# Hybrid diffusion layer on one core: gate loads issued ahead, two buffers for the S5 output rows, a freer engine choice for weight low parts

## The chip, the cores and the metric

The kernel runs on one core of a Trainium2 chip. The metric is the device time of one launch in microseconds. Three runs of the kernel before gave 1892.18, 1900.79 and 1914.18 us, median 1900.79 us. The engines are named as in the profile: PE (TensorE matmul), PEld (its weight loads), DVE (VectorE), ACT (ScalarE), POOL (GpSimd), and SP (SyncE), whose queue issues the DMAs; SPq is that queue.

## The reference, cut to what matters

One layer over 512 latent tokens with a context of 256 tokens, width 1024: half-step SwiGLU FFN, then two token mixers side by side (a bidirectional S5 state-space scan and a bidirectional RWKV-7), merged by per-channel gates, then a second half-step FFN and a final RMSNorm. The part around the change:

```python
xs = scan of h[c] = a * h[c-1] + x[c]            # S5, both directions
ya = (ya_f + ya_b) + p['s5_D'] * u
ya = jax.nn.gelu(ya)
ya = ya * jax.nn.sigmoid(ya @ p['s5_w_glu'])
...
yb = (yb * g) @ p['rwkv_w_o']
merged = jax.nn.sigmoid(gate_a) * (ya @ p['s5_w_proj']) + jax.nn.sigmoid(gate_b) * yb
return merged @ p['w_out']
x = x + mod_x[5] * out_x
```

## The kernel before, in words

**Products in three parts.** Every dense weight block of 128 x 1024 floats is loaded as `raw`, rounded by ACT into a high part `wh`, and the rest `wl = raw - wh` is formed by DVE or POOL. Activations are held the same way (for instance `yg`, `ya`, `yb`, `hx`, each a pair). `mm3` then issues three matmuls per 128-row block: wh x high, wh x low, wl x high. The blocks form one long list `self.items`, worked off in order by the generator `dense` (line 352): split the item's weights, issue loads for free `raw` buffers, split a few items ahead (four among the products of the mixers, two elsewhere), then issue the matmuls. `w_split` (line 328) picks the engine for `wl`: from item `n_post + 2` up to `n_ffn`, which is wo, wproj and wout, always POOL; in the other items DVE where a modelled comparison (`late`) says that POOL would end later.

**The order.** All instructions are emitted by one planner (`Plan`, line 52), which models when each engine becomes free and runs a set of generators by priority: a generator gives up its turn with the list of things it next needs, and the planner resumes the first one in priority whose needs are met at its modelled PE time. So the order in each engine's queue is fixed at build time by the model; on the chip each engine works its queue strictly in that order. `dense` is the filler: it runs where nothing of higher priority is ready, or where the modelled PE work of the last stretch falls under a quota.

**Stage b2** (`phase_b2`, line 1817; about 1109 to 1332 us). Beside one another: `rw_main` and `rw_pre` (RWKV chunks 4 to 11), `rw_solve` for two groups of triangular solves on DVE (results `Tl`, `AT` stored in `ti`, read back as `T` and `tt`), `s5_rec` (line 1747), which is 63 steps of four small POOL operations on `t` and `hs`, then `s5_out` (line 1765), eight blocks of PE work (`b<-U,Tz`, `b<-hs,gt`) that store their rows to `yd` in DRAM, and the filler with the sigmoid gates: `gst` goes to `gates` in DRAM.

**After it.** `s5_post` (line 1962) reads `yd` back tile by tile into `yi` (one buffer), applies the gelu into `ga` and splits it into `yg`. `glu_mm` (line 1888) needs all four `yg` tiles and gives `ya`. Four gate items stand behind it in the list. Then come sixteen items of two products each, one product being 12 matmuls of 256 columns into one PSUM bank: `wo_mm` for the first half of the tokens (reads `yb`), `proj_mm` for the first half (reads `ya`), then both for the second half. Each product loads its gate tile `gt` (128 x 256) from `gates` just before its matmuls are issued; `gt` has two buffers. DVE multiplies it with the bank (`gb` for wo, `gt` itself for wproj); for wproj it also adds `gb`, ACT rounds to the high part of `hx`, and DVE subtracts for the low part. The products rotate over four PSUM banks. `wout_mm` follows from `hx`. The second FFN starts near 1500 us.

Of the kernel before, what the change touches and what calls it, by code (L numbers as in the profile page):

```python
# [8 lines left out]
F32 = mybir.dt.float32  # L9
# [274 lines left out]
class Kern:  # L284
# [43 lines left out]
    def w_split(self):  # L328

        nc, i = self.nc, self.n_split  # L330
        if i == len(self.items):
            return
        s = next((s for s in self.slots if i < self.end[s[0]]), None)
        if s is None:
            return
        if i not in self.raw:
            self.w_loads(1)
        self.n_split += 1
        nb = self.items[i][1]
        r, sr = self.raw.pop(i)  # L340
        self.slots.remove(s)
        wh, wl = (s[0].tile([128, 8, 128], F32R, name=n, tag=f"{n}{s[1]}") for n in ("wh", "wl"))
        nc.scalar.copy(wh[:, :nb], r[:, :nb])
        f = self.sch.free
        late = max(f["P"], self.sch.t) + 2300 > max(f["V"], self.sch.t) + 1150
        eng = nc.vector if (i < self.n_post + 2 or i >= self.n_ffn) and late else nc.gpsimd
        eng.tensor_sub(wl[:, :nb], r[:, :nb], wh[:, :nb].bitcast(F32))
        if sr[0] not in self.gone:
            self.raws.append(sr)
        self.wsp[i] = (wh, wl, s)  # L350
# [48 lines left out]
    def build(self):  # L399
        nc, tc, a, es = self.nc, self.tc, self.a, self.es  # L400
        self.X, self.C = X, C = Reg(0, NX, 4), Reg(1, NCT, 0)
        self.raw, self.wsp, self.n_load, self.n_split, self.late = {}, {}, 0, 0, None
        self.slots, self.raws, self.gone, self.end, self.items = [], [], set(), {}, []
        per = es.enter_context(self.pool("per"))
# [46 lines left out]
        i = self.n_gate + GATE0  # L451
# [1295 lines left out]
    def s5_rec(self, r):  # L1747

        Pg, h = self.nc.gpsimd, r.hs
        yield [f"s5in{r.s}"]  # L1750
        if not r.v:
            Pg.tensor_copy(h[:, 0], self.s5e)
        for c in range(1, 32 if r.v else 64):
            t1 = r.sp.tile([128, 2, 32], F32, name="t1")
            t2 = r.sp.tile([128, 2, 32], F32, name="t2")
            Pg.tensor_mul(t1, self.arr, h[:, c - 1])
            Pg.tensor_mul(t2, self.aii, h[:, c - 1, ::-1])
            Pg.tensor_add(t1, t1, h[:, c])
            Pg.tensor_add(h[:, c], t1, t2)
            yield [("P", RECP)]  # L1760
        if r.v:
            Pg.tensor_copy(self.s5e, h[:, 31])
        self.sch.post(f"s5rec{r.s}")
# [106 lines left out]
    def dbank(self):  # L1870
        self.alt += 1
        return self.bank(self.dbanks[self.alt % len(self.dbanks)])

    def wo_mm(self, h, t, wh, wl):
        nc, c = self.nc, self.X.half[h]
        for e in range(2):
            d = 2 * t + e
            yield [f"yb{h}2", f"yb{h}3"]
            yield [self.yb[1][:, :, c]]
            g = self.cp.tile([128, 256], F32, name="gt", bufs=2)  # L1880
            nc.sync.dma_start(g, self.gates[8 + d][:, c])
            px = self.dbank()[:, 0:256]
            for k in range(4):
                self.mm3(px, wh[:, e * 4 + k], wl[:, e * 4 + k], self.yb[0][:, k, c], self.yb[1][:, k, c], k == 0, k == 3)
                yield
            nc.vector.tensor_mul(self.gb[:, d], g, px)
# [19 lines left out]
    def proj_mm(self, h, t, wh, wl):  # L1906
        nc, cp, c, late = self.nc, self.cp, self.X.half[h], None
        for e in range(2):
            d = 2 * t + e
            g = cp.tile([128, 256], F32, name="gt", bufs=2)  # L1910
            nc.sync.dma_start(g, self.gates[d][:, c])
            px = self.dbank()[:, 0:256]
            for k in range(4):
                self.mm3(px, wh[:, e * 4 + k], wl[:, e * 4 + k], self.ya[0][:, k, c], self.ya[1][:, k, c], k == 0, k == 3)
                yield
            nc.vector.tensor_mul(g, g, px)
            nc.vector.tensor_add(g, g, self.gb[:, d])
            hi, lo = (x[:, d, c] for x in self.hx)
            nc.scalar.copy(hi, g)
            if late:  # L1920
                nc.vector.tensor_sub(*late)
            late = lo, g, hi.bitcast(F32)
            if e:
                nc.vector.tensor_sub(*late)
# [37 lines left out]
    def s5_post(self, pb):  # L1962

        nc = self.nc
        yield ["yd3", "sv"]
        self.sos.close()
        self.s5s.close()
        self.c1 = c = pb.enter_context(self.pool("c1"))
        R = lambda n: [c.tile([128, 4, NX], F32R, name=f"{n}{i}") for i in range(2)]
        self.ga, self.yg, self.ya, self.yb = c.tile([128, 4, NX], F32, name="ga"), R("yg"), R("ya"), None  # L1970
        for t in range(4):
            yi = c.tile([128, 8, 64], F32, name="yi", bufs=1)
            nc.sync.dma_start(yi, self.yd[t].rearrange("(t o) g c -> (o g) t c", o=16))
            yield [yi]
            for o, i, n in ((0, 16, 48), (48, 0, 16)):
                nc.scalar.activation(self.ga[:, t, o * 8:(o + n) * 8].rearrange("p (c t) -> p c t", t=8),
                                     yi[:, :, i:i + n].rearrange("p t c -> p c t"), AF.Gelu_apprx_tanh)
            self.hl(c, self.ga[:, t], self.yg[0][:, t], self.yg[1][:, t])
            self.sch.post(f"yg{t}")
# [159 lines left out]
```

## Time and profile before

| what | value |
|---|---|
| median of three runs | 1900.79 us (1892.18 to 1914.18) |
| profiled execution, its own time | 1891.72 us |
| its span, first to last instruction | 1890.0 us |
| PE busy | 1672.3 us (88%) |
| DVE / ACT / POOL busy | 996.4 / 716.9 / 687.5 us |
| mean granted PE clock | 0.939 of full speed |
| chain that ended last | PE 56%, DVE 14%, DMA 14%, ACT 6%, issue 4% |

A row of the chain of waits gives its start, its length, and the engine or DMA that held it. A row of a timeline gives start, length, engine, operation and tiles, and in brackets how long the engine stood idle before it and what released it. Nearly all instructions carry one line number, that of the helper that records them (L209), so rows are told apart by tile names.

### The profile page before, as it was taken

Reading aid. Unit: us, or ns where it says so; the run is one execution under the profiler, and the core shown is the slowest. Engines: PE = TensorE matmul, PEld = TensorE weight load, DVE = VectorE, ACT = ScalarE, POOL = GpSimd, SP = SyncE. Lnnn points to the kernel's source line nnn. Section 1 sums busy time; section 2 is a strip of 40 time slices with the busy share of each in tenths; the row PEclk is TensorE's granted clock in tenths of the full one; section 3 lists DMA queues with packets and bytes.
Section 4 is the critical chain, followed back from the end, with each engine's and each line's share of the span. In section 5 each row is a group of like instructions: output and inputs, shape, how many; then the busy total and the mean of one; then the engine's idle time right before and its main releaser. Section 6 shows DMA issues by size and latency. Waiting matters only on the chain.

```text
span 1890.0 us, 33157 instructions
## 1 busy us (share of the span) xinstructions
PE 1672.3 (88%) x13208; PEld 1400.3 (74%) x13208; DVE 996.4 (53%) x1747; ACT 716.9 (38%) x1200; POOL 687.5 (36%) x815
## 2 busy tenths in 40 slices
PE   6889999999999988778976789968697999999996
PEld 3689987778878867665544567758587988888886
DVE  3376564755558728355788855643343433333335
ACT  3355442545463212535443333443443332222222
POOL 0144231555764314621334537660065421111111
PEclk9999999999999999888988889979799999999998
DMA  9955541335454474433753566466364223323231
GB/s 310 331 167 195 183 155 57 113 106 159 143 160 140 141 190 151 119 123 128 252 160 105 148 223 188 118 172 176 123 215 159 67 69 101 99 91 101 98 101 56
DMA packets 235626, 278.43 MB, mean 147 GB/s; under 512 B 93616, under 2 KB 186800, under 8 KB 234448
## 3 DMA queue, kind: packets, MB, share of 16 engines
q1 hardware_dynamic: 235472, 276.32, 47.8%
q8 instruction: 104, 1.70, 0.4%
q14 instruction: 50, 0.41, 0.1%
HBM read 234.31 MB, written 43.22 MB: 147 GB/s over the span
## 4 chain that ended last, share of the span: by engine, by line
PE 56%; DVE 14%; DMA 14%; ACT 6%; issue 4%; POOL 3%; SPq 3%; DVEq 0%; ACTq 0%; POOLq 0%
PE b L209 56%; DMA wmod<-in_wmod 3%; SPq L209 3%; POOL wl L209 2%; ACT wh L209 2%; DMA Hd<-H 2%; DMA raw<-in_wgu 2%; DVE st L209 1%; DVE mh L209 1%; DVE wl L209 1%; DMA gt<-gates 1%; DVE rs L209 1%; DVE prod L209 1%; DVE cvr L209 1%; DVE H L209 1%
## 5 line engine op out<-in xcount | busy, mean ns | idle before, releaser
L209 PE MATMUL b<-hx,wh 128*128 128x512 f32 (+1 forms) x2432 | 698.2, 374 | 22.6 <-ACT wh L209 10.9
L209 POOL TENSOR_TENSOR wl<-raw,wh 128x1024 fp32r<-128x1024 f32 x135 | 329.3, 2443 | 822.0 <-ACT wh L209 748.1
L209 PEld LDWEIGHTS b<-hx,wh 128*128 128x128 f32 x2432 | 439.1, 194 | 106.7 <-issue 19.0
L209 PE MATMUL b<-hx,wl 128*128 128x512 f32 (+1 forms) x1216 | 448.6, 369 | 7.6 <-POOL wl L209 6.0
L209 ACT CAST wh<-raw 128x1024 fp32r<-128x1024 f32 x273 | 283.1, 1046 | 196.3 <-DMA raw<-in_wgu 69.8
L209 DVE TENSOR_TENSOR wl<-raw,wh 128x1024 fp32r<-128x1024 f32 x138 | 187.3, 1358 | 276.9 <-ACT wh L209 274.5
L209 PEld LDWEIGHTS b<-hx,wl 128*128 128x128 f32 x1216 | 235.7, 194 | 47.9 <-POOL wl L209 8.6
L209 PE MATMUL b<-ah,wh 128*128 128x512 f32 (+1 forms) x560 | 196.8, 351 | 3.6 <-ACT wh L209 2.0
L209 PE MATMUL b<-ah,wl 128*128 128x512 f32 (+1 forms) x560 | 194.9, 348 | 1.9 <-POOL wl L209 1.9
L209 PE MATMUL b<-al,wh 128*128 128x512 f32 (+1 forms) x560 | 194.7, 348 | 0.0
L209 PE MATMUL b<-hc,wh 128*128 128x256 f32 x928 | 173.1, 287 | 1.2 <-ACT hc L209 1.2
L209 PEld LDWEIGHTS b<-hc,wh 128*128 128x128 f32 x928 | 145.8, 192 | 10.9 <-issue 8.2
L209 PE MATMUL b<-hc,wl 128*128 128x256 f32 x464 | 131.7, 284 | 0.0
L209 PEld LDWEIGHTS b<-ah,wh 128*128 128x128 f32 x560 | 108.0, 193 | 16.6 <-ACT wh L209 2.2
L209 PEld LDWEIGHTS b<-ah,wl 128*128 128x128 f32 x560 | 107.9, 193 | 15.2 <-POOL wl L209 2.1
L209 ACT CAST ah<-prod 128x512 fp32r<-128x512 f32 (+1 forms) x68 | 36.6, 538 | 212.6 <-DVE prod L209 212.5
L209 PEld LDWEIGHTS b<-al,wh 128*128 128x128 f32 x560 | 107.8, 192 | 12.1
L209 ACT ACTIVATE sil<-b 128x512 f32<-128x512 f32 (+1 forms) x68 | 35.0, 515 | 149.8 <-PE b L209 149.6
L209 PEld LDWEIGHTS b<-hc,wl 128*128 128x128 f32 x464 | 89.3, 192 | 0.0
L209 DVE TENSOR_TENSOR prod<-sil,b 128x512 f32<-128x512 f32 (+1 forms) x68 | 39.6, 582 | 93.0 <-PE b L209 74.4
L209 DVE SCALAR_TENSOR_TENSOR x1c<-b,gp,x1c 128x512 f32<-128x512 f32 (+1 forms) x67 | 43.9, 662 | 81.2 <-PE b L209 81.2
L209 PE MATMUL b<-wmod,zs 128*32 128x256 f32 x576 | 54.3, 465 | 19.3 <-DMA wmod<-in_wmod 19.1
(289 smaller groups left out, 2331.0 us busy)
## 6 DMA issues: line engine op xcount, KB each, us to landing
raw<-in_wgu SPq DMA_DIRECT2D x132, 512.0 KB, 3.9
wmod<-in_wmod SPq DMA_DIRECT2D x72, 512.0 KB, 5.3
raw<-in_wdn SPq DMA_DIRECT2D x66, 512.0 KB, 3.7
raw<-in_win SPq DMA_DIRECT2D x49, 512.0 KB, 4.0
gt<-GTd SPq DMA_DIRECT2D x32, 256.0 KB, 3.8
abk<-st SPq DMA_DIRECT2D x8, 1024.0 KB, 5.5
AB<-abk SPq DMA_DIRECT2D x8, 1024.0 KB, 6.3
GTd<-gst SPq DMA_DIRECT2D x16, 256.0 KB, 2.4
```

The costliest lines, as they stand in the source:

```text
L209: r = f(out, *args, **kw)
```

## The change

Four edits. `w_split` may give any item's `wl` to DVE: it does so where `late` holds, and always while `s5_rec` of the latent tokens is being emitted (`self.rec`). The gate tiles come from a new method `gate(n)`, which issues the loads of products n, n+1 and n+2 as far as not yet issued, in the order in which the products use them; they have four buffers in the pool `c1` instead of two in `cp`. `yi` shares the ring `sg` of two buffers, which `glu_mm` uses later, instead of one buffer of its own.

```diff
     def w_split(self):
...
         late = max(f["P"], self.sch.t) + 2300 > max(f["V"], self.sch.t) + 1150
-        eng = nc.vector if (i < self.n_post + 2 or i >= self.n_ffn) and late else nc.gpsimd
+        eng = nc.vector if late or self.rec else nc.gpsimd
...
     def s5_rec(self, r):
...
         if not r.v:
+            self.rec = True
             Pg.tensor_copy(h[:, 0], self.s5e)
         for c in range(1, 32 if r.v else 64):
...
             yield [("P", RECP)]
+        self.rec = False
...
+    def gate(self, n):
+
+        order = [(h, m + 2 * t + e) for h in range(2) for m in (8, 0) for t in range(4) for e in range(2)]
+        while len(self.gts) < min(n + 3, len(order)):
+            h, d = order[len(self.gts)]
+            self.gts.append(self.c1.tile([128, 256], F32, name="gt", bufs=4))
+            self.nc.sync.dma_start(self.gts[-1], self.gates[d][:, self.X.half[h]])
+        return self.gts[n]
...
     def wo_mm(self, h, t, wh, wl):
...
-            g = self.cp.tile([128, 256], F32, name="gt", bufs=2)
-            nc.sync.dma_start(g, self.gates[8 + d][:, c])
+            g = self.gate(16 * h + d)
...
     def proj_mm(self, h, t, wh, wl):
...
-            g = cp.tile([128, 256], F32, name="gt", bufs=2)
-            nc.sync.dma_start(g, self.gates[d][:, c])
+            g = self.gate(16 * h + 8 + d)
...
     def s5_post(self, pb):
...
-            yi = c.tile([128, 8, 64], F32, name="yi", bufs=1)
+            yi = c.tile([128, 8, 64], F32, name="yi", tag="sg", bufs=2)
```

`build` also sets `self.rec = False` and `self.gts = []`.

## Rows read from the trace of the kernel before

**Rows 1.** Windows by stage; columns: stretch, length, busy time of each engine (count), PE clock, DMA

```profile
1240.00:1253.00 13.00, 0.28 (x2) 0.18 (x2) 5.39 (x14) 1.93 (x1) 11.58 (x38) 0.58 0.29 94
...
1332.00:1352.00 20.00, 6.75 (x11) 2.79 (x11) 3.89 (x6) 10.22 (x16) 1.26 (x1) 0.56 0.38 100
...
1389.00:1420.00 31.00, 26.36 (x203) 25.01 (x201) 12.77 (x26) 10.38 (x14) 20.82 (x9) 0.99 0.69 228
1420.00:1456.00 36.00, 27.37 (x196) 26.50 (x197) 13.90 (x34) 11.15 (x17) 18.82 (x8) 0.91 0.55 176
```

**Rows 2.** Chain of waits, 1389 to 1457 us: start, length, what held it

```profile
1392.84 3.70 DMA gt<-gates
...
1407.31 3.12 PE b L209 x24
...
1430.58 4.01 DMA gt<-gates
...
1455.53 1.55 PE b L209 x11
```

**Rows 3.** Groups of PE instructions, 1389 to 1464 us: busy, mean, idle before and releaser

```profile
L209 PE MATMUL b<-yb,wh 128*128 128x256 f32 x128 | 26.6, 308 | 7.6 <-DVE gb L209 4.5 <-DVE gt L209 3.1
L209 PE MATMUL b<-ya,wh 128*128 128x256 f32 x128 | 23.8, 287 | 3.2 <-DVE gt L209 2.7 <-DVE gb L209 0.5
...
L209 PE MATMUL b<-hx,wh 128*128 128x256 f32 (+1 forms) x49 | 9.1, 286 | 2.5 <-DVE gt L209 2.5
```

**Rows 4.** Timeline of POOL, one split of the wproj stretch

```profile
1412.76 2.36 POOL L209 TENSOR_TENSOR wl<-raw,wh 128x1024 fp32r<-128x1024 f32 x1 [5.53 <-ACT wh L209]
```

**Rows 5.** Timeline of DVE beside it, one wproj item

```profile
1413.94 0.42 DVE L209 TENSOR_TENSOR gt<-gt,b 128x256 f32<-128x256 f32 x1 [1.75 <-DMA gt<-gates]
1414.40 1.00 DVE L209 TENSOR_TENSOR gt<-gt,gb 128x256 f32<-128x256 f32 x1
...
1416.11 0.98 DVE L209 TENSOR_TENSOR hx<-gt,hx 128x256 fp32r<-128x256 f32 x2
```

**Rows 6.** Timeline of ACT: two gelus of S5 rows, and one split

```profile
1336.93 1.15 ACT L209 ACTIVATE ga<-yi 128x384 f32<-128x384 f32 x2
1338.12 0.62 ACT L209 CAST yg<-ga 128x512 fp32r<-128x512 f32 x1
1341.09 1.15 ACT L209 ACTIVATE ga<-yi 128x384 f32<-128x384 f32 x2 [2.36 <-DMA yi<-yd]
...
1411.64 1.04 ACT L209 CAST wh<-raw 128x1024 fp32r<-128x1024 f32 x1
```

**Rows 7.** Groups of PE instructions, 1335 to 1392 us

```profile
L209 PE MATMUL b<-yg,wh 128*128 128x512 f32 x32 | 14.3, 517 | 13.3 <-ACT yg L209 13.3
```

**Rows 8.** Chain of waits, 1332 to 1352 us: the first of four loads

```profile
1332.47 2.93 DMA yi<-yd
```

**Rows 9.** Window 1109 to 1259 us, instructions on wl alone: PE, PEld, DVE, POOL

```profile
1109.00:1259.00 150.00, 38.68 (x96) 18.50 (x95) 9.98 (x8) 12.17 (x5) 0.90 0.54 158
```

**Rows 10.** Waits, 1100 to 1260 us: total, times, longest

```profile
POOL wl L209 <- ACT wh L209: 20.7, 5, 8.0
```

**Rows 11.** Timeline of POOL in the S5 recurrence

```profile
1173.13 1.30 POOL L209 TENSOR_TENSOR t<-aii,hs 128x64 f32<-128x64 f32 x1
...
1219.34 0.32 POOL L209 TENSOR_TENSOR hs<-t,t 128x64 f32<-128x64 f32 x1
...
1220.69 0.32 POOL L209 TENSOR_TENSOR hs<-t,t 128x64 f32<-128x64 f32 x1
...
1261.15 0.32 POOL L209 TENSOR_TENSOR hs<-t,t 128x64 f32<-128x64 f32 x1
```

**Rows 12.** Timeline of DVE at the same moment as the first of these

```profile
1173.01 1.24 DVE L209 TENSOR_TENSOR wl<-raw,wh 128x1024 fp32r<-128x1024 f32 x1 [3.21 <-ACT wh L209]
```

**Rows 13.** Timeline of PE: the wait for the solves, and the first S5 output block

```profile
1252.33 0.28 PE L209 MATMUL b<-T,M 32*32 32x32 f32 x2 [12.51 <-DMA T<-ti]
...
1267.88 2.50 PE L209 MATMUL b<-hs,gt 64*64 64x64 f32 x64
```

More of the change, by code (lines that the diff above doesn't have):

```diff
@@ L401, in build @@
         self.X, self.C = X, C = Reg(0, NX, 4), Reg(1, NCT, 0)
+        self.rec = False
+        self.gts = []
         self.raw, self.wsp, self.n_load, self.n_split, self.late = {}, {}, 0, 0, None
@@ L1760, in s5_rec @@
             yield [("P", RECP)]
+        self.rec = False
         if r.v:
```

## The prediction

> **What bounds the kernel now.** I read the windows by stage first, then the chain of waits inside the stages where PE is not full, then the timelines of the engines that the chain names. PE is busy for 88% of the span, so only the stretches where it stands can give anything. Nothing before the latent recurrence (about 1109 us) is touched by the diff: until then `rec` is false and the old rule and the new one give the same engine. Behind 1500 us the rule is the same too. Between them three stretches stand out in the windows [rows 1]. From 1389 to 1456 us, the sixteen wo and wproj items, PE is busy 53.7 of 67 us. From 1332 to 1352 us it is busy 6.75 of 20, at a granted clock of 0.56. From 1240 to 1253 us it does nothing, clock 0.58.
>
> In the first stretch the chain runs from one gate load to the next: issue, up to 4.0 us until it lands, a DVE multiply, the next load [rows 2]. PE waits 13.3 us in all (7.6 + 3.2 + 2.5), each time for DVE to empty one of the four banks [rows 3], and DVE in turn waits for `gt`: with two buffers a load can only start when the product two before has been read. In the second stretch PE waits for `yg` [rows 7]; ACT waits 2.36 us for each further `yi`, because its single buffer is refilled only after the gelu has read it [rows 6]. In the third, PE waits 12.51 us for the solves' result [rows 13], with no other work in its queue.
>
> **Part A, gates and `wl` in wo and wproj.** Removed: the loop load, multiply, load. The same 32 loads go out, two products earlier. A load for product n+2 now waits on SP for the reads of product n-2; behind it on SP stand the raw weight loads and the next gate loads. It has three products to land, 3 x 1.5 = 4.5 us by the 3.12 us that 24 matmuls take [rows 2], against at most 4.01 us of landing, so SP's wait costs PE nothing unless the landings grow beyond that. The floor is then PE alone: from 1389 us, where wo begins, to 1455.5 us, where PE runs through again [rows 2], are 66.5 us; 16 items at 3.0 us plus an estimated 1.3 us for the last RWKV gating products in the same queue are 49.3, so at most 17 us can go.
>
> What is late next is DVE in wproj. An item's two products cost it two multiplies of 0.42, two adds that take about 0.43 each when nothing else holds them, 0.98 for the two subtractions [rows 5], and some 0.35 us of waiting for ACT's cast: 3.0 us, no more than PE. On top comes the split. On POOL it takes 2.36 us [rows 4], and one add that began inside it took 1.00 us and ended only after it [rows 4, 5]; POOL's 2.36 and the 1.84 us of adds and subtractions then exclude one another, 4.2 us an item. On DVE it takes 9.98 / 8 = 1.25 us [rows 9] and waits at the head of DVE's queue until ACT has made `wh` (1.04 us [rows 6], of which about 0.6 is not covered by the last subtraction): with the next item's multiply behind it, 5.0 us an item. The rule `late` will alternate, as the engine that just took a split counts as busy; I take the middle, 4.6 us. PE may lead DVE by four banks, two items, and in wo DVE has 0.84 + 1.25 us an item and catches up. So of each half's lag some 2.2 us reach PE. Sum: 49.3 + 0.5 (the first gate still lands after PE has filled its banks) + 2 x 2.2 = 54.2, a gain of 12.3 us. Ends: 17 (all hidden) and 4 (every split in wproj on DVE, below).
>
> The Trainium skill, SBUF — State Buffer, section "SBUF: two separate sides", says that a DVE instruction with two SBUF inputs and a GpSimd instruction exclude each other for the whole of the instruction that starts first. The trace agrees at both places where I looked: the add of 1.00 us beside POOL's split, and POOL's operation of 1.30 us beside DVE's split, where its neighbours take 0.32 [rows 4, 5, 11, 12]. By that rule alone, with every wproj split on POOL, DVE would need 4.2 us an item and the part would give about 13 us.
>
> **Part B, `yi`.** The four loads keep their size and queue. The second is issued right behind the first instead of after the first gelu. First: issued 1332.47, landed after 2.93 us [rows 8], gelu 1336.93 to 1338.08, cast to 1338.74 [rows 6]. Second: already there, gelu 1338.74 to 1339.89, cast to 1340.5. Third: its load waits for the first gelu (1338.1), lands at 1341.1, cast done 1342.9. Fourth: waits for the second gelu (1339.9), lands 1342.85, cast done 1344.7. Before, one tile followed the other after 4.16 us (1336.93 to 1341.09 [rows 6]), so the fourth cast ended near 1351.1. Gain 6.4 us, all on PE's path, since PE waits 13.3 us for `yg` [rows 7]. The loads behind on SP (x1c and four raw blocks) move earlier by as much. `sg` in `glu_mm` waits for reads that are over by then: nothing. If PE had other work up to 1345 this gain would go into part C's.
>
> **Part C, `rec`.** Five splits leave POOL's queue in the recurrence: 12.17 us of work [rows 9] and 20.7 us of idling at their heads for `wh` [rows 10]. They go to DVE, where each may hold up a POOL operation by about 1.0 us (1.30 against 0.32 [rows 11, 12]): 5 us back. A free step takes 1.35 us [rows 11], so the last `hs`, at 1261.5 us, would come at about 1261.5 - 32.9 + 5 = 1234. What PE does earlier is set by the planner's order. Its own costs for a removed split (928 + 145 ns for `wh`, 2300 for `wl`) are about 3.4 us, five times 17 us: by so much the eight S5 output blocks move up in PE's queue, the first from 1267.9 [rows 13] to about 1250 or into the empty 13 us from 1240. Two blocks fit there (2.50 us each [rows 13] and the 16 matmuls ahead of it): about 6 us of PE work in time that was empty. The rest ends up to 17 us earlier, so the remaining 6.9 us of the `yg` wait (13.3 - 6.4) get RWKV work beside them. Together 13 us, which I take. Ends: from below, nothing of this and 5 x 1.25 = 6.3 us more on DVE before the solves' results, on which PE waits, so a loss of 6; from above 19.6, all that PE stands in the two windows besides part B (12.7 + 13.25 - 6.4 [rows 1]). DVE is busy only 5.39 of the 13 us before the solves' result [rows 1], so the upper end is the nearer one, and 13 lies on its side of the middle. What a steadier PE gains in clock (0.56 and 0.58 of full speed in those windows, near the lower level of 1.2 GHz) is not counted; it is why the range reaches below the best case.
>
> **Sum.** 12.3 + 6.4 + 13 = 31.7 us. The profiled execution took 1891.72 us (span 1890.0, some 1.7 us around it), so 1860.0 us on its scale. The median of the runs shown, 1900.79, is 0.48% above it; on that scale the forecast is 1869 us.
>
> **The rivals.**
> 1. Part C gives nothing: the solves on DVE and the wait for `T` govern the stage, or the planner's order hardly moves. For it: PE's longest wait there is the 12.51 us for `T`, not for `hs` [rows 13]. Against it: the S5 blocks all come after it, and the `yg` wait is theirs. 1891.7 - 18.7 = 1873.0, on the median's scale 1882.
> 2. DVE binds wproj: all splits land there, 5 us an item and the gates are no longer the limit but nothing else is gained. Part A gives 4, the sum 23.4: 1877 us. For it: `late` starts in DVE's favour by 1150 ns. Against it: after a wproj item DVE's modelled queue is longer than that.
> 3. All of PE's idle time in the three stretches closes: 17 + 6.4 + 19.6 = 43 us, 1858 us. For it: the idle time is there. Against: the RWKV chunks still follow one another after the result of the solves at 1252 [rows 13].
> 4. Slower: S5 output stands in PE's queue before the recurrence is done on the chip, and the RWKV chunks behind it wait. Part C's 1234 us holds 63 steps; DVE operations of two SBUF inputs stretch them [rows 11, 12]. If each took 0.64 us more than there, the last would come 40 us later, at 1274; if PE arrives at 1239 it stands 35 us, 13 of which it stood anyway. 22 - 18.7 = 3.3 us slower: 1895.0, or 1904. It decides from 0.58 us a step on (18.7 + 13 us of standing); against it stand the free steps of 1.35 us, and that 8 of the stretch's 13 splits [rows 9] were DVE's already.
> 5. The change does not do what it says: `yi` loads are emitted behind other waits and stay serial. Then 25.3 us, 1875 us.
>
> **How the numbers follow.** Forecast 0.43; rival 1 0.25; rival 2 0.10; rival 3 0.08; rival 4 0.10; rival 5 0.04. About 1% (19 us) is what a measurement of this kernel can tell from no change. Rival 1 lies on that edge, two thirds of it inside (0.17); with half of rival 4 and a little of the rest, same is 0.24; slower by more is the other half of rival 4, 0.05; faster 0.71. The range leaves out rival 4 and reaches some 10 us past rivals 1 and 3: 1848 to 1892.
>
> **What would show each step.** A right: the stretch from the first wo matmul to the first wout matmul takes 52 to 57 us, `gt<-gates` all but leaves the chain there, and DVE carries about half of the 24 splits. B right: the four gelus start 2 us apart after the first pair, not 4.1. C right: no `wl` on POOL between the first and last `hs`, last `hs` near 1235, S5 output blocks beside the wait for `T`, and less than 7 us of waiting for `yg`. The prediction is wrong if PE waits for `hs`, if the wait for `T` grows by more than 5 us, or if a wproj item still takes about 5 us on DVE.

## The result and the profile after

The changed kernel takes 1881.82 us, median of 20 runs (1874.13 to 1899.37); the kernel before takes 1903.05 us in its 20 (1892.18 to 1914.18). The ratio is 0.9893, with a 95% interval of 0.9874 to 0.9913: 1.07% faster, some 20 us. The forecast was 1869 us; rival 1 (parts A and B work, part C gives nothing) had 1882.

The profiled execution took 1882.93 us, its span 1881.2 us, at a granted clock of 0.935. From the page: the busy row of the engines, then the two groups of `wl` (16 of the 135 splits on POOL are gone, 16 more are on DVE).

```profile
PE 1681.7 (89%) x13208; PEld 1409.2 (75%) x13208; DVE 1008.5 (54%) x1763; ACT 716.1 (38%) x1200; POOL 655.1 (35%) x799
...
L209 POOL TENSOR_TENSOR wl<-raw,wh 128x1024 fp32r<-128x1024 f32 x119 | 292.2, 2457 | 805.7 <-ACT wh L209 748.4
...
L209 DVE TENSOR_TENSOR wl<-raw,wh 128x1024 fp32r<-128x1024 f32 x154 | 213.2, 1385 | 291.0 <-ACT wh L209 288.7
```

All kernels here have the same instructions in the same order up to the first POOL operation of the latent recurrence (`hs<-s5e`), yet in single profiled runs that operation started anywhere from 1109.85 us (before) to 1127.64 us. So I compare stage lengths from that operation on, each cut at a named instruction, and leave totals to the repeated runs. Stages in which two kernels have the same order differ by up to some 3 us between profiles, sums of several stages by up to some 5 us. Lengths go from start to start.

| us | before | after |
|---|---|---|
| recurrence, first to last `hs` on POOL | 154.0 | 134.6 |
| its start to first S5 output block (PE `b<-hs,gt`) | 158.0 | 160.3 |
| that block to the first gelu | 69.0 | 66.7 |
| first gelu to last `yg` cast | 13.5 | 7.1 |
| last `yg` cast to first wo matmul | 38.7 | 40.0 |
| first wo to first wout matmul | 66.3 | 56.2 |
| first wout matmul to the end | 434.5 | 435.4 |
| start of recurrence to first wout matmul | 345.7 | 330.3 |

Two stages give the gain, 10.1 us in wo and wproj and 6.4 us at the gelus. Their sum of 16.5 us lies at the lower end of what the repeated runs say (some 17 to 24 us); the profiled execution of before took 1891.72 us, less than any of its 20 runs, so what is left is not placed in a stage. The recurrence is 19.4 us shorter, and nothing behind it comes sooner.

The windows of after, with the columns of [rows 1]: the stretch with the wait for T and the first two chunks, the one up to the gelu, the gelus, and wo with wproj.

```profile
1250.00:1275.75 25.75, 14.56 (x312) 13.06 (x312) 8.60 (x20) 8.14 (x14) 0.32 (x1) 0.67 0.63 182
1275.75:1342.41 66.66, 55.24 (x1352) 49.41 (x1348) 21.36 (x45) 26.18 (x59) 1.26 (x1) 0.98 0.57 162
1342.41:1349.56 7.15, 4.77 (x8) 2.21 (x9) 2.08 (x3) 6.38 (x12) 0.00 (x0) 0.50 0.57 152
...
1389.54:1445.79 56.25, 49.48 (x387) 48.35 (x385) 40.16 (x65) 21.24 (x30) 20.47 (x8) 0.94 0.72 237
```

Part B, the timeline of ACT in after, against [rows 6]: the gelus start 1.7, 2.5 and 1.7 us apart, and only the third still waits for its load.

```profile
1342.41 1.15 ACT L209 ACTIVATE ga<-yi 128x384 f32<-128x384 f32 x2
...
1344.12 1.19 ACT L209 ACTIVATE ga<-yi 128x384 f32<-128x384 f32 x2
...
1346.60 1.18 ACT L209 ACTIVATE ga<-yi 128x384 f32<-128x384 f32 x2 [0.65 <-DMA yi<-yd]
...
1348.34 1.19 ACT L209 ACTIVATE ga<-yi 128x384 f32<-128x384 f32 x2
```

Part A, the chain of waits of after over the same items as [rows 2]. Where before stepped from load to load, PE now carries the chain for 13.67 us at a time. Landings of gate loads that PE notices are left at two places: the first of all, 6.35 us, and those at the start of the second half. The three landings make 15.5 us of the chain, where gate loads had 20.2 us before.

```profile
1393.23 6.35 DMA gt<-gates
...
1400.15 13.67 PE b L209 x96
...
1425.55 3.16 DMA gt<-gates
...
1430.37 6.02 DMA gt<-gates
...
1437.06 9.09 PE b L209 x73
```

Part C, the timeline of PE in after, against [rows 13]: the last `hs` began at 1250.03 us, 9 us before T was there, but the first S5 output block stands behind two groups of T,M products, as before.

```profile
1259.41 0.28 PE L209 MATMUL b<-T,M 32*32 32x32 f32 x2 [12.12 <-DMA T<-ti]
...
1274.52 0.69 PE L209 MATMUL b<-T,M 32*32 32x32 f32 x32
1275.14 0.69 PE L209 MATMUL b<-U,Tz 128*64 128x64 f32 x16
1275.75 2.51 PE L209 MATMUL b<-hs,gt 64*64 64x64 f32 x64
```

### The profile page after: what moved, and what is told of

Its sections match the earlier page's. It is cut to its first block, busy times and chain, and to the rows that moved or that the text cites. A ratio compares the mean times of both kernels' runs of the same rounds, so it can differ in the third digit from the quotient of the medians.

```text
span 1881.2 us, 33153 instructions
## 1 busy us (share of the span) xinstructions
PE 1681.7 (89%) x13208; PEld 1409.2 (75%) x13208; DVE 1008.5 (54%) x1763; ACT 716.1 (38%) x1200; POOL 655.1 (35%) x799
## 5 line engine op out<-in xcount | busy, mean ns | idle before, releaser
L209 PE MATMUL b<-hx,wh 128*128 128x512 f32 (+1 forms) x2432 | 704.6, 377 | 19.0 <-ACT wh L209 10.6
L209 POOL TENSOR_TENSOR wl<-raw,wh 128x1024 fp32r<-128x1024 f32 x119 | 292.2, 2457 | 805.7 <-ACT wh L209 748.4
L209 PEld LDWEIGHTS b<-hx,wh 128*128 128x128 f32 x2432 | 444.4, 197 | 103.7 <-issue 16.2
L209 DVE TENSOR_TENSOR wl<-raw,wh 128x1024 fp32r<-128x1024 f32 x154 | 213.2, 1385 | 291.0 <-ACT wh L209 288.7
L209 PEld LDWEIGHTS b<-ah,wl 128*128 128x128 f32 x560 | 107.4, 192 | 13.5 <-POOL wl L209 0.5
```

The lines of the kernel that those rows point to most:

```text
L209: r = f(out, *args, **kw)
```

## The experiments

Ratios are to the kernel before, run on the same chip in the same series, with 95% intervals. Theory: A and B work by the loads alone, C fails because the order of PE's queue hardly moves. Rivals: `late` brings a share of A; C's sooner recurrence is worth something by itself; or it is hidden by the chain behind T.

### One part at a time

**e_yi**, only the shared buffers of `yi`, on the kernel before:

```diff
-            yi = c.tile([128, 8, 64], F32, name="yi", bufs=1)
+            yi = c.tile([128, 8, 64], F32, name="yi", tag="sg", bufs=2)
```

> Only the two buffers for the rows of S5. If the trace of the changed kernel is read rightly, the four gelus come 1.7 to 2.5 us apart instead of 4.1, and the whole is 6 us shorter (ratio to the kernel before 0.997). Rival: PE finds other work or another wait there, and the ratio is 1.000.

Measured: 0.9960 [0.9934, 0.9986]; gelu to last cast 7.1 us, wo to wout 65.8. Part B is there alone, with its whole 6.4 us.

**e_late**, only the freer engine rule (without `rec`), on the kernel before:

```diff
-        eng = nc.vector if (i < self.n_post + 2 or i >= self.n_ffn) and late else nc.gpsimd
+        eng = nc.vector if late else nc.gpsimd
```

> Only the free engine choice outside the recurrence (no rec, old gate loads, old S5 rows). If the gate loads bind wo and wproj, the stretch from the first wo matmul to the first wout matmul stays at 62 to 66 us (before 66.3) and the ratio is 0.998 to 1.000. Rival: the splits on POOL bind it; then it falls to 58 us and the ratio is 0.996.

Measured: 1.0022 [1.0000, 1.0045]; wo to wout 70.6 us, 4.3 more than before. The waits of PE in that stretch sum to 17.0 us, where before had 13.3 [rows 3]:

```profile
PE b L209 <- DVE gt L209: 9.4, 6, 3.5
PE b L209 <- DVE gb L209: 7.6, 6, 4.2
```

Both expectations missed: the stage is longer than either had it. Without the loads ahead, the rule costs time in this stage; in the whole the interval begins at no change.

**e_rec**, only the splits of the recurrence on DVE, on the kernel before:

```diff
-        eng = nc.vector if (i < self.n_post + 2 or i >= self.n_ffn) and late else nc.gpsimd
+        eng = nc.vector if (i < self.n_post + 2 or i >= self.n_ffn) and late or self.rec else nc.gpsimd
```

> Only the splits of the recurrence on DVE. If the planner's order holds the S5 output blocks behind the wait for T, POOL ends the recurrence 15 to 20 us sooner, PE's first S5 output block stands where it stood, and the ratio is 1.000 (0.999 to 1.002). Rival: some of the 20 us that the medians show comes from here; ratio 0.996 or less.

Measured: 0.9989 [0.9970, 1.0008]; recurrence 135.0 us instead of 154.0, start to first S5 output block 157.9, to the first wout matmul 346.1 (before 345.7). The recurrence is 19 us shorter and PE is served no sooner.

**u_wl**, the changed kernel with the old engine rule, so gates ahead and `yi` alone:

```diff
-        eng = nc.vector if late or self.rec else nc.gpsimd
+        eng = nc.vector if (i < self.n_post + 2 or i >= self.n_ffn) and late else nc.gpsimd
```

> The changed kernel with the old rule for the engine (all splits of wo and wproj on POOL, none forced to DVE): gate loads ahead and the S5 rows alone. If the loads were what bound wo and wproj, that stretch takes 56 to 58 us and the ratio is 0.991 to 0.993. Rival: without DVE's help POOL binds, one split of 2.4 us an item that excludes DVE's adds: 61 us or more, ratio 0.995.

Measured: 0.9878 [0.9855, 0.9901]; wo to wout 53.5 us, of which PE is busy 49.1 at full clock (the window below; after had 0.94). That is better than both expectations. With the low parts taken as before it is no slower than the changed kernel, and this stage is 2.7 us shorter.

```profile
1403.89:1457.38 53.49, 49.13 (x393) 47.75 (x392) 31.31 (x58) 21.42 (x30) 37.64 (x16) 1.00 0.74 242
```

**u_rec**, the changed kernel without `rec`:

```diff
-        eng = nc.vector if late or self.rec else nc.gpsimd
+        eng = nc.vector if late else nc.gpsimd
```

> The changed kernel without the splits' move to VectorE during the recurrence of the latent tokens (the engine rule for wo, wproj and wout stays as changed). Theory (the sooner end of the recurrence buys nothing, since the S5 output stands behind the wait for T in either order): recurrence 154 us instead of 135, start of the recurrence to the first wout block unchanged within 1.5 us at 329 to 332, ratio 0.988 to 0.991. Rival (it is worth something, by a shorter POOL queue or by the order behind it): 335 us or more, ratio 0.992 or above.

Measured: 0.9898 [0.9876, 0.9920]; recurrence 154.1 us, start to first wout matmul 333.5, between the two expectations, with a ratio as the theory had it. The ratio is that of the changed kernel within 0.05%. Taken out or put in alone, part C shows no effect beyond the intervals, some 0.2%.

### What the engine rule costs in wo and wproj

**x_early**, the changed kernel with the first gates' load issued one step sooner:

```diff
     def glu_mm(...):
         if t == 1:
+            self.gate(0)
             self.sch.post("glu")
```

> The changed kernel, with the first gates' load issued one step sooner, before glu's splits are posted, so that no raw weight load stands ahead of it in SP's queue. Theory (the new engine rule costs 2.7 us in wo and wproj because splits taken early by VectorE free raw buffers, and their loads then go ahead of the first gate loads): the first gates land before PE needs them, PE's 4.5 us wait for the first gated tile goes, and wo to wout takes 51.5 to 53 us instead of 56.2: ratio 0.986 to 0.988. Rival (the splits at the head of VectorE's queue delay the sigmoid's adds and evacuations themselves): wo to wout stays at 55 to 56 us, ratio 0.989.

Measured: 0.9866 [0.9833, 0.9899]; wo to wout 52.8 us, as the theory had it. DVE's first gate multiply now starts at 1394.10 us without waiting, 6.2 us behind the first wo matmul; in after it was 10.1. First after, then x_early, in DVE's timeline:

```profile
1399.67 0.79 DVE L209 TENSOR_TENSOR gb<-gt,b 128x256 f32<-128x256 f32 x2 [3.90 <-DMA gt<-gates]
```

```profile
1394.10 0.74 DVE L209 TENSOR_TENSOR gb<-gt,b 128x256 f32<-128x256 f32 x2
```

PE's wait for `gb` falls from 6.0 us (longest 4.5) to 2.3 us (longest 1.0), as the waits of PE in after and then in x_early show:

```profile
PE b L209 <- DVE gb L209: 6.0, 3, 4.5
```

```profile
PE b L209 <- DVE gb L209: 2.3, 3, 1.0
```

The splits stay on DVE, so they were not the cost in themselves. The first gate load is issued 3.7 us after the first wo matmul in after and 3.6 us in u_wl, but took 6.35 us to land in the one and 3.75 in the other. Three raw loads of 512 KB each stand ahead of it in after (issued from 1388.77 us, 0.8 us before wo starts; in u_wl from 1401.13, 2.8 us before), besides one more right before it in both. That they are what delayed it is inferred from this order; that its lateness was the price is shown. SP's timeline of after, then of u_wl:

```profile
1388.77 1.34 SPq L209 DMA_DIRECT2D raw<-in_wproj  x3
...
1393.23 1.97 SPq L209 DMA_DIRECT2D gt<-gates  x4
```

```profile
1401.13 2.75 SPq L209 DMA_DIRECT2D raw<-in_wproj  x3
...
1407.52 1.87 SPq L209 DMA_DIRECT2D gt<-gates  x4
```

The wait cost more than its own length. Right behind it, from 1400.15 to 1404.16 us, PE's granted clock was 0.50 in after, the lower of its two levels, and 19 matmuls took 4.0 us, 0.21 us each where those behind them took 0.12. In x_early the clock stayed at 1.00 over the whole stage, and PE is busy 47.9 us in it instead of 49.5:

```profile
1387.89:1440.67 52.78, 47.91 (x386) 46.46 (x385) 40.39 (x65) 21.25 (x30) 20.41 (x8) 1.00 0.74 246
```

**u_wl_early**, the same line added to u_wl.

> Gates and yi as changed, the old engine rule for the low parts, and the first gates' load one step sooner. Theory (the first gates are late there too, though less): wo to wout 50.5 to 52 us instead of 53.5, ratio 0.985 to 0.987. Rival (PE is busy 49 of those 53.5 us already, and its first wait there ends on yb and not on the gates): 53 to 54 us, ratio 0.988 as without it.

Measured: 0.9879 [0.9850, 0.9909]; wo to wout 53.8 us. The rival: where the first gates were not late, the sooner load gives nothing.

**x_pdve**, the changed kernel with more of wproj's splits on DVE:

```diff
+        proj = self.n_post + 2 <= i < self.n_ffn - 8 and (i - self.n_post - 2) // 4 % 2
-        eng = nc.vector if late or self.rec else nc.gpsimd
+        eng = nc.vector if late or self.rec or proj else nc.gpsimd
```

> The changed kernel, with every low part of wproj's weights taken by VectorE where the changed one lets either engine take it. By the prediction's bounds a wproj item then costs VectorE 5.0 us (add, multiply, evacuation and split one after the other) against 3.9 us of PE's work, so VectorE binds: eight items of 5.0 for 3.9, wo to wout 62 to 66 us instead of 56.2, ratio 0.992 to 0.995. Rival (without GpSimd on the shared port the add falls from 2.2 us to about 0.9, so the item stays at 4 us): 55 to 58 us, ratio 0.989.

Measured: 0.9903 [0.9875, 0.9931]; wo to wout 56.8 us, in the rival's range. But the case that the theory priced did not come about. DVE has 11 splits of this stretch instead of 7, so the four low parts of wproj that POOL still had have moved. A split is made some four items ahead of its products, though: wproj's fall beside wo's products, and beside wproj's own products lie the splits of the second half of wo and of wout, 5 of them still on POOL. The stage gives no verdict on a split on DVE beside every wproj item, but its rows price one item of each kind. From DVE's timeline of x_pdve, an item with its split on DVE, and below it the last add of a later item; the second fence is the split on POOL that lay beside that add.

```profile
1443.76 1.23 DVE L209 TENSOR_TENSOR wl<-raw,wh 128x1024 fp32r<-128x1024 f32 x1
1444.90 0.42 DVE L209 TENSOR_TENSOR gt<-gt,b 128x256 f32<-128x256 f32 x1
...
1446.14 0.43 DVE L209 TENSOR_TENSOR gt<-gt,gb 128x256 f32<-128x256 f32 x1
1446.49 0.98 DVE L209 TENSOR_TENSOR hx<-gt,hx 128x256 fp32r<-128x256 f32 x2
...
1452.85 2.19 DVE L209 TENSOR_TENSOR gt<-gt,gb 128x256 f32<-128x256 f32 x1
```

```profile
1452.26 2.50 POOL L209 TENSOR_TENSOR wl<-raw,wh 128x1024 fp32r<-128x1024 f32 x1 [1.75 <-ACT wh L209]
```

With the split on DVE the item takes 3.7 us (1443.76 to 1447.47) and each add 0.43. With POOL's split beside it, the second add takes 2.19, and items follow each other after 4.25 us (1451.61 to 1455.86). POOL's row shows what closes that circle: 2.50 us of split and 1.75 us of waiting for `wh`, which ACT casts behind the `hx` of the add that was held.

### What holds the S5 output back

**x_rx500**, the changed kernel with a cost in the planner that lets it end the latent recurrence sooner:

```diff
-            yield [("P", RECP)]
+            yield [("P", RECP if r.v else 500)]
```

> The changed kernel, with 500 in place of 0 as the planner's cost of a GpSimd step of the recurrence of the latent tokens (it sets the order of instructions alone; every instruction is the same). Theory (the S5 output stays behind the wait for T because the planner, by its own costs, ends the recurrence just after its modelled gap is over): now the model ends it 13 us earlier, inside that gap, so the first S5 output block stands before the second T,M group in PE's queue and runs near its last hs; from the start of the recurrence to that block 140 to 147 us instead of 160.3, the wait for T 3 to 8 us instead of 12.1, and 6 to 12 us less in all: ratio to before 0.982 to 0.986, where the changed kernel had 0.989. Rival (the way from the solves to T and on through the RWKV chunks sets the end, not S5's output): the block moves, the wait for T shrinks, and the chunks behind it end as much later: ratio 0.988 to 0.991.

Measured: 0.9901 [0.9873, 0.9928]. The first S5 output block comes 10 us sooner (150.3 us from the start of the recurrence), behind one group of T,M products instead of two; but the wait for T is unchanged, and the stage to the first gelu is 10.6 us longer, so that the first wout matmul stands at 330.7 us. Timeline of PE, and the window up to the gelu:

```profile
1260.59 0.28 PE L209 MATMUL b<-T,M 32*32 32x32 f32 x2 [12.20 <-DMA T<-ti]
...
1268.79 2.50 PE L209 MATMUL b<-hs,gt 64*64 64x64 f32 x64
```

```profile
1268.79:1346.07 77.28, 64.53 (x1544) 58.29 (x1540) 27.54 (x54) 27.12 (x61) 1.26 (x1) 0.96 0.57 152
```

As in the rival, an exchange behind T gives nothing; the wait for T, which both expected to shrink, did not. That the block could be put ahead of T by this cost was wrong.

**x_s5o0**, the S5 output ahead of the RWKV streams in priority:

```diff
-S5O = 2
+S5O = 0
```

> The changed kernel, with the S5 output's stream placed ahead of the RWKV streams in the planner's order (priority 0 in place of 2). Theory (PE has work of both kinds after the wait for T, and the end is set by whichever is last, here S5's output with its gelus and casts): the last yg cast comes 10 to 15 us sooner, the RWKV chunks 5 to 10 us later, 3 to 8 us less in all: ratio 0.985 to 0.988. Rival (it is a mere exchange: PE's queue is full from T on, so what S5 gains the chunks lose): start of the recurrence to the first wout block stays at 330 us, ratio 0.988 to 0.991; should the chunks' chain bind, 0.992 or more.

Measured: 0.9933 [0.9908, 0.9957], as the rival had it for a binding chain of chunks; nominally worse than the changed kernel, whose interval it just touches. The first gelu comes 11.3 us sooner (215.7 us after the start of the recurrence instead of 227.0), but from the last cast to wo it now takes 52.3 us instead of 40.0. The chunks are late instead, and PE waits for a load that had been no matter:

```profile
PE b L209 <- DMA U<-udx: 7.8, 3, 4.4
```

**x_o8**, the order forced: the first latent T,M group is emitted only after two S5 output blocks:

```diff
-            yield [M, t1]
+            yield [M, t1] + (["yd0"] if p == 8 else [])
```

> The changed kernel, with one wait more in the planner alone: the T,M group of the first latent chunk (that which waits 12 us for T) is placed only after the first two S5 output blocks; no instruction is added or changed. The sooner end of the recurrence (some 9 us ahead of T) can now be used: the two blocks, 3.2 us each with their U,Tz products, run inside the wait for T. Theory (from T to the gelus PE is the limit, so work taken out of that stretch shortens it): the wait for T falls from 12.1 to 5 to 6.5 us, start of the recurrence to the first gelu 221 us instead of 227, and to the first wout block 323 to 326 instead of 330: ratio to before 0.985 to 0.987 where the changed kernel has 0.989. Rival (the chain of RWKV chunks behind T sets the end of that stretch, and the S5 blocks lie in its gaps already): the wait shrinks, but the stage ends as before, 329 to 331 us, ratio 0.988 to 0.991.

Measured: 0.9915 [0.9886, 0.9945]; start to first wout matmul 332.2 us. Neither expectation, nearest to the rival's. The blocks do stand ahead of T in PE's queue, but they wait too, for `U`. Timeline of PE:

```profile
1257.71 1.12 PE L209 MATMUL b<-U,Tz 128*64 128x64 f32 x16 [17.72 <-DMA U<-udx]
1258.76 2.56 PE L209 MATMUL b<-hs,gt 64*64 64x64 f32 x64
...
1265.22 0.69 PE L209 MATMUL b<-T,M 32*32 32x32 f32 x32
```

The last `hs` had been there since 1248.2 us. SP's timeline and its longest wait show why: the loads of the S5 output stand behind the stores of the solve's result, and SP stood 15.6 us until DVE had it.

```profile
1246.01 0.33 SPq L209 DMA_DIRECT2D ti<-Tl  x1
...
1250.72 0.30 SPq L209 DMA_DIRECT2D T<-ti  x1
...
1253.04 0.43 SPq L209 DMA_DIRECT2D U<-udx  x1
```

```profile
SPq L209 <- DVE Tl L209: 15.6, 1, 15.6
```

The T,M group starts 152.1 us after the start of the recurrence (after: 144.0), and from it to wo takes 124.9 us instead of 130.1. So two blocks taken out of that stretch shorten it by 5.2 us of their 6.4, and the late `U` costs 8.1: the blocks begin 144.6 us after the start, when T is there as well, and only then delay it. Whether the 5.2 us would be left as a gain with `U` and the other S5 loads issued before the solves was not tried.

**b_o8**, x_o8 and x_early together:

> The changed kernel with both edits: the two S5 output blocks ahead of the first latent T,M group, and the first gates' load one step sooner. If the two gains lie in different stages they add: 6 us at the wait for T and 3.4 us in wo and wproj, start of the recurrence to the first wout block 320 to 323 us, ratio 0.982 to 0.984. If the S5 blocks gain nothing: 326 to 327 us and 0.986 to 0.988, as with the sooner load alone.

Measured: 0.9870 [0.9845, 0.9894]; wo to wout 52.7 us, start to first wout matmul 333.7. With the order of x_o8 up to wo, T,M starts 154.5 us after the start and wo 126.5 us behind it: again later by more (10.5 us) than the stretch is shorter (3.6 us). Only the early load's gain is in it: a second kernel in which wo and wproj are 3.5 us shorter.

The lowest ratio of all is x_early's, 0.9866; its interval overlaps that of the changed kernel, so the runs' times alone don't tell the two apart.

## Why the prediction was right, and where not

The direction was right, and the time lies inside the range. Against 1869 us it is 13 us more, about the size of part C's term, of which the runs show nothing. That the total meets rival 1's 1882 us to the microsecond is luck in part: A fell 2.2 us short, the longer series of before has a median 2.3 us higher than the three runs, and the runs show some 4 us more than the stages.

**A: the loads were the limit, as forecast; several terms were off.** 56.2 us against 54.2. PE's own work was put at 49.3 us and measured 49.5, of which some 1.6 are the stretch at the lower clock. The step "the first gate still lands after PE has filled its banks", 0.5 us, measured 4.5 us of waiting for `gb`: landings, bounded by the 4.01 us of before, reached 6.35. The lag of DVE in wproj, put at 2 x 2.2 us, reached PE with 1.5 at most: 0.95 us in the second half's wo and 0.54 early in its wproj, both on banks that waited for `gb`. No wait of PE for `gt` is left in this stretch. (49.5 + 4.5 + 1.5, and 0.7 for one `wh`, make the 56.2.)

The item of 4.2 us with POOL's split came out (4.24 in after, for instance the multiplies at 1417.75 and 1421.99), but not by its sum. I let POOL's 2.36 us and 1.84 us of adds and subtractions exclude one another. The rows show one add locked out, while the rest of the item runs beside an idle POOL, which waits 1.75 us for `wh`; that 1.75 is near 1.84 is luck. The lock itself is what the Trainium skill says in SBUF — State Buffer, section "SBUF: two separate sides": a DVE instruction with two SBUF inputs and a GpSimd instruction exclude each other for a whole instruction. The adds of 2.19 us beside POOL's split and 0.43 without agree. The item of 5.0 us with the split on DVE was too dear; the rows say 3.7. And `late` was no part of the gain: gates ahead give all of it (53.5 us with the old rule), and the rule takes 2.7 back by the late first gates.

**B: right**, 6.4 us forecast and measured (13.5 to 7.1), alone and with the rest.

**C: the step that failed is "by so much the eight S5 output blocks move up in PE's queue".** I took the planner's saved cost, 17 us, for the shift. Worked through, the planner's model ends the recurrence 9 us sooner (POOL free at 1239.0 instead of 1248.1), but its own gap around the first latent T,M group closes at 1235.3; from there the RWKV streams, of higher priority, fill PE, and the model places the first S5 output block only 2.6 us sooner (1248.9 instead of 1251.5). These are the planner's own times, read as the kernels are built. Nor would a better order have been enough: x_o8 shows that the loads of the S5 output stand behind the solve in SP's queue, which I had not looked at. The third lock is PE's work itself: from T to the gelu it was exchanged, not saved (x_rx500, x_s5o0).

The recurrence itself was put at 124 us from its start (1234) and took 134.6. The row that I took for its last `hs` in before, at 1261.15 us, is the last but two; the last one began at 1263.85, 154.0 us from the start. Of the 32.9 us taken away from these [rows 9, 10], 13.5 came back. Some 4.8 are POOL's next operation on `Tl`, which now waits 12.8 us for the store of the solve instead of 8.0, as the waits of POOL in before and then in after show. Some 7.5 are the 252 operations of the recurrence, which take 396 ns on the mean instead of 366, where I had allowed 5. About 1 us is not assigned.

```profile
POOL Tl L209 <- DMA ti<-Tl: 8.0, 1, 8.0
```

```profile
POOL Tl L209 <- DMA ti<-Tl: 12.8, 1, 12.8
```

**The rivals.** 1 is what happened, for both of the reasons it named, and for SP's queue. 2 fell: PE waits 0.5 us in wproj. 3 and 4 fell with C; PE never waited for `hs`. 5 fell with e_yi.

**The signs I gave.** 52 to 57 us, the splits shared between the engines (DVE has 11 of the 24), the gelus 2 us apart and no `wl` on POOL in the recurrence came true. That `gt<-gates` all but leaves the chain in wo and wproj did not: 15.5 us of it are left, of 20.2. A last `hs` near 1235 us, S5 blocks beside the wait for T, and less than 7 us of waiting for `yg` did not (7.7 us, of 13.3).

## What to carry to other kernels

When an order is fixed by a model at build time, a faster engine moves work only as far as the model's own gaps and priorities allow: work the model through before you count a shift. Then follow each operand of the moved work to the queue that loads it, since an in-order DMA queue behind a long wait holds it just as the engine's own order does. A prefetch is worth what its first load allows: look at what stands ahead of that one.

## What was not expected of the hardware

An operation that all these kernels reach by the same instructions started up to 18 us apart in single profiles (1109.85 to 1127.64 us), as much as the whole effect; stage lengths agreed within about 3 us. The start goes with TensorE's granted clock on the way there: 0.93 on the mean in before, which was the earliest, and 0.90 in e_late, the latest; over all 14 profiles the two go against one another with a correlation of -0.91. The 20 runs of the changed kernel show it in their totals, 1874.13 us at a granted clock of 0.936 and 1899.37 us at 0.922. Why the clock differs between runs of the same instructions is not shown.

And DVE's add of 0.43 us became 1.84 to 2.19 us in after where it began inside POOL's split, yet PE paid at most 1.5 us for it in wo and wproj, with four banks between the two engines.
